# Eight-expert layer of a decoder trunk: gather, scatter and one-hot transposes cut into single steps between blocks of products

## The chip, the cores and the metric

The kernel runs on one core of a Trainium2 chip. The metric is the device time of one execution in microseconds (us); the time before is the median of three executions. Engines are named as the profile names them: PE is TensorE (PEld its weight loads), DVE is VectorE, ACT is ScalarE, POOL is GpSimd, SP is SyncE, which issues the weight loads from memory.

## What is computed

A two-layer decoder trunk on 256 tokens of width 1024. The change lies in the second layer's channel mixer alone, a mixture of eight experts with two experts for each token:

```python
def moe_swiglu(x, w_router, w_gate, w_up, w_down):
    ...
    gates = jnp.sum(jax.nn.one_hot(top_i, N_EXPERTS, dtype=jnp.float32) * top_w[..., None], axis=1)
    y = jnp.zeros((B * S, D), jnp.float32)
    for e in range(N_EXPERTS):
        y = y + gates[:, e:e + 1] * swiglu(xt, w_gate[e], w_up[e], w_down[e]).astype(jnp.float32)
    return y.astype(x.dtype).reshape(B, S, D)
```

`swiglu` is `(silu(x @ w_gate) * (x @ w_up)) @ w_down`, with an inner width of 3584. All numbers are float32.

## The kernel before, in words

**Products.** A float32 weight is split into a rounded part and the rest: ACT writes `whi` (L151), DVE writes `wlo` = weight - `whi` (L152), 128x2048 elements at a time. Three `whi` and three `wlo` buffers exist, so a split waits until PE has used the one three before it. The activations are split in the same way.

**Blocks.** `gate_up(e, m)` takes 512 of an expert's 3584 inner columns: two gate splits, two up splits (g0, g1, u0, u1 below), and after it `down(e, m-1)` takes the two splits d0, d1 of the down matrix of the block before. So a block, written (e, m) with e from 0 to 7 and m from 0 to 6, has six splits on ACT and on DVE and three groups of products on PE; (e, 0) ends with the last `down` of expert e-1. An expert with at most 64 tokens takes the branch `light()` in `either` (16 products for each group, lines L870 and L943 and a `fold` product L836), the others `heavy()` (24 for each group, L161 to L163). With these inputs experts 0, 3, 5 and 6 are heavy and 1, 2, 4 and 7 light, as the lines on PE show; expert 0 has no branch.

**Small work in a block.** ACT: `silu` of the gate bank (L892), the copies `fl` for the fold (L849), half of the transposed inner activations (`wk<-ht`, L915). DVE: `hh` = up times silu (L898) and the other half `wk` (L917). PE: four transposes `ht` (L166). `defer(n, fn)` puts a function on the list `later`; `msplit` takes 2 off n for every 128x2048 split and calls what has reached 0, so such a copy stands behind a later split on its engine's queue.

**Work of an expert or a pair.** `gather(pr)` makes the one-hot masks `pm` of two experts and their inputs `xg` by products with the masks (`gx`, L741): 8 half parts of 4 products, each into one PSUM bank, of which DVE copies the columns of the first expert (L747) and ACT those of the second (L749). It is called whole at the end of block (e, 3) of an odd expert. `gather2` turns the masks round (`gsb`, L790 and L792), copies the gates' column on DVE (`gs`, L793) and the turned masks on ACT (`pTm`, L794). `scaled` and `scatter` multiply the expert's result by its gate (ACT L964, DVE L965, written into `wk`) and add it to the tokens' rows by 8 products (`sc`, L973 and L974) and 4 additions on DVE (`r<-r,sc`, L979); `post` calls it in the middle of block (e+1, 1), before `turn` writes `wk` again.

**PSUM.** The pool `acc` has four banks: two hold an expert's `y` all the time, the other two serve `ht`, `gx`, `gsb` and `sc` in turn. The Tile framework orders each engine's instructions and sets all semaphores; in the built program ACT's copy of a bank waits for DVE's copy of the same bank (`xg` L749 for L747, `pTm` for `gs`).

Of the kernel before, what the change touches and what calls it, by code (L numbers as in the profile page):

```python
# [46 lines left out]
SILU_N, MULT_N, HT_N, FOLD_N = 4, 4, 4, 2  # L47
# [39 lines left out]
def trunk(ctx: ExitStack, tc: tile.TileContext, x, consts, mconsts, vecs, lnrows, w_in, w_uq, w_ukv, w_o,  # L87
# [549 lines left out]
    def moe(pool, raws2, raws3, r, gb, rw):  # L637
# [87 lines left out]
        def gather(pr):  # L725
            pm = pool.tile([P, 2, 256], F32R, tag="pm", name="pm")
            for tt in range(2):
                for j in range(2):
                    ip = nc.vector.tensor_scalar(pm[:, tt, j * P:(j + 1) * P], iota, posm[:, tt, 2 * pr + j:2 * pr + j + 1],
                                            None, ALU.is_equal)  # L730
            if pr == 0:
                hold_splits(((), None, 2), ((pw,), nc.gpsimd, 2), ((i1, pw), nc.gpsimd, 1), ((i1, ip), None, 3))
            xgs = [pool.tile([P, KD, P, 2], F32R, tag="xg", name="xg", bufs=3) for j in range(2)]

            def part(k2):
                for hl, src in enumerate((xth, xtl)):
                    b = bank(acc, "gx")
                    for kk in range(2):
                        k = 2 * k2 + kk
                        for tt in range(2):  # L740
                            nc.tensor.matmul(b[:, kk * 256:(kk + 1) * 256], src[:, tt, k * P:(k + 1) * P], pm[:, tt, :],  # L741
                                             start=(kk == 0 and tt == 0), stop=(kk == 1 and tt == 1))
# [8 lines left out]
            return pm, xgs, part  # L751
# [26 lines left out]
        def gather2(pr, pm, xgs):  # L778
            gs = pool.tile([P, 2], F32, tag="gs", name="gs")
            pT = pool.tile([P, 2, 2, P], F32R, tag="pTm", name="pTm")  # L780

# [5 lines left out]
            for j in range(2):  # L787
# [5 lines left out]
                nc.vector.tensor_copy(gs[:, j:j + 1], b[:, 256 + 2 * pr + j:257 + 2 * pr + j])  # L793
                nc.scalar.copy(pT[:, j, :, :], b[:, 0:256].rearrange("p (a b) -> p a b", b=P))  # L794
            return [(gs[:, j:j + 1], pT[:, j]) for j in range(2)]
# [3 lines left out]
        def defer(n, fn):  # L799
            later.append([n, fn])  # L800
# [37 lines left out]
        def gate_up(e, m, xg, part=None, mid=None):  # L838
# [12 lines left out]
            for g, w in enumerate((e_gate, e_up)):  # L851
# [29 lines left out]
                if dyn:  # L881
                    if g == 0 or (e, m) != LAST:
                        defer(FOLD_N, lambda g=g: copy_for_fold(g))
                    else:
                        copy_for_fold(g)
                if g == 0:
# [7 lines left out]
                    defer(SILU_N + dyn, silu)  # L894
# [64 lines left out]
        def scaled(yb, gs, swap):  # L959
            ys_ = []  # L960
            for n in range(2):
                o = 1024 * (n if swap else 1 - n)
                yh, yl = [wk[:, o + 512 * i:o + 512 + 512 * i] for i in range(2)]
                nc.scalar.activation(yh, yb[n], AF.Copy, scale=gs)  # L964
                nc.vector.scalar_tensor_tensor(yl, yb[n], gs, yh.bitcast(F32), ALU.mult, ALU.subtract)  # L965
                ys_.append((yh, yl))
            return ys_

        def scatter(e, ys_, pT):
            for n in range(2):  # L970
                for tt in range(2):
                    b = bank(acc, "sc")
                    nc.tensor.matmul(b, pT[:, tt, :], ys_[n][0], start=True, stop=False)  # L973
                    nc.tensor.matmul(b, pT[:, tt, :], ys_[n][1], start=False, stop=True)  # L974
                    if e == NE - 1:
                        ln_sum(ya[tt], ya[tt], {n: b}, fsums[tt], 1.0, (n,))
                    else:
                        cs = slice(n * 512, (n + 1) * 512)
                        nc.vector.tensor_tensor(ya[tt][:, cs], ya[tt][:, cs], b, ALU.add)  # L979
# [79 lines left out]
        post = prev = None  # L1059
# [6 lines left out]
        def finish(e, m, ht, fold_up=None, fe=None, hook=None):  # L1066
            nonlocal post
# [3 lines left out]
            if m == FM - 1:  # L1071
                gs, pT = sc[e // 2][e % 2]
                ys_ = scaled(yb[e], gs, e == NE - 1)
                post = lambda: scatter(e, ys_, pT)

        for e in range(NE):
            pr = e // 2
            for m in range(FM):

                def mid():  # L1080
                    nonlocal post
# [14 lines left out]
                if prev is not None:  # L1096
                    h2 = [ht[0]]

# [4 lines left out]
                    finish(*prev[:2], ht[0], fold_up, e, hook if (e, m) == LAST else None)  # L1103
                if m == 3 and e == NE - 1:
# [3 lines left out]
                if m == 3 and e % 2 == 1 and e < NE - 1:  # L1108
                    half[pr + 1] = gather(pr + 1)
                    for k2 in range(4):  # L1110
                        half[pr + 1][2](k2)
                prev = (e, m, hh)
        finish(*prev[:2], h2[1])
        post()
# [248 lines left out]
```

## Time and profile before

| what | us |
|---|---|
| median of three executions | 1484.8 (1484.56 to 1489.42) |
| the profiled execution | 1489.02 |
| its span | 1486.9 |
| PE busy | 1368.8 (92%) |
| DVE busy | 1177.1 (79%) |
| ACT busy | 994.1 (67%) |

The table's last four rows are one execution, taken by the hardware profiler; a share of busy time is an average over stages with different limits. The expert stage lies between about 490 and 1472 us of the span. The rows further down are read block by block: each window begins at one group of PE's products and ends at the same group of the next block.

### The profile page before, as it was taken

What the parts mean: (1) busy time and instruction counts of PE and PEld (TensorE: products, weight loads), DVE (VectorE), ACT (ScalarE), POOL (GpSimd) and SP (SyncE); (2) the same over time, 40 slices, a digit from 0 to 9 for tenths busy, and PEclk for the clock granted to TensorE, in tenths of its full rate; (3) what the DMA queues carried; (4) which work ended last, traced back from release to release, by engine and by line L of the source; (5) the groups of instructions that cost most, each with busy time, mean ns of one, the idle gap of its engine ahead of it and who ended that gap; (6) DMA issues with size and microseconds to landing.
All of it is one profiled execution on the core that took longest, in us unless ns stands there. A gap on an engine that the chain in (4) does not pass through costs nothing. (4 is left out here: it accounts for less than half of the span.)

```text
span 1486.9 us, 18580 instructions
## 1 busy us (share of the span) xinstructions
PE 1368.8 (92%) x6927; PEld 1131.7 (76%) x6927; DVE 1177.1 (79%) x1264; ACT 994.1 (67%) x1065; POOL 79.8 (5%) x113
## 2 busy tenths in 40 slices
PE   7999999999998899988889998998989899999895
PEld 6987999998986788766666777876668787887663
DVE  6577655556667888898999976889987787888996
ACT  3564444445655677777879865778867677778884
POOL 3012000003103000000000000000000000001001
PEclk8999999999999999999999999999999999999997
DMA  6733554544525789998999987989999797999980
GB/s 258 276 132 113 199 197 174 197 144 146 207 86 227 256 327 359 374 380 322 419 372 419 419 321 268 355 331 397 419 368 345 258 367 288 358 367 372 357 351 30
DMA packets 63513, 429.46 MB, mean 289 GB/s; under 512 B 7058, under 2 KB 7570, under 8 KB 15268
## 3 DMA queue, kind: packets, MB, share of 16 engines
q1 hardware_dynamic: 63364, 427.81, 75.1%
q8 instruction: 81, 1.33, 0.4%
q14 instruction: 36, 0.29, 0.1%
q0 software_dynamic: 32, 0.03, 0.0%
HBM read 426.76 MB, written 1.05 MB: 288 GB/s over the span
## 5 line engine op out<-in xcount | busy, mean ns | idle before, releaser
L152 DVE TENSOR_TENSOR wlo<-raw,whi 128x2048 fp32r<-128x2048 f32 (+4 forms) x475 | 910.3, 1937 | 170.5 <-ACT whi L151 164.9
L151 ACT CAST whi<-raw 128x2048 fp32r<-128x2048 f32 (+4 forms) x482 | 772.3, 1619 | 295.3 <-PE eg L163 45.5
L871 PE MATMUL eg<-wlo,xg 128*128 128x512 f32 x448 | 182.5, 407 | 11.6 <-DVE wlo L152 9.5
L162 PE MATMUL eg<-wlo,xg 128*128 128x512 f32 x448 | 179.4, 400 | 7.7 <-DVE wlo L152 7.7
L161 PE MATMUL eg<-whi,xg 128*128 128x512 f32 x448 | 181.0, 404 | 0.0
L870 PE MATMUL eg<-whi,xg 128*128 128x512 f32 x448 | 179.7, 401 | 0.8 <-ACT wk L915 0.8
L163 PE MATMUL eg<-whi,xg 128*128 128x512 f32 x448 | 178.6, 399 | 0.0
L871 PEld LDWEIGHTS eg<-wlo,xg 128*128 128x128 f32 x448 | 85.2, 190 | 45.5 <-DVE wlo L152 29.4
L162 PEld LDWEIGHTS eg<-wlo,xg 128*128 128x128 f32 x448 | 88.3, 197 | 25.3 <-DVE wlo L152 8.6
L943 PE MATMUL y<-wlo,wk 128*128 128x512 f32 x224 | 95.7, 427 | 11.3 <-DVE wlo L152 10.0
L163 PEld LDWEIGHTS eg<-whi,xg 128*128 128x128 f32 x448 | 88.1, 197 | 17.7
L161 PEld LDWEIGHTS eg<-whi,xg 128*128 128x128 f32 x448 | 88.3, 197 | 16.7
L584 PE MATMUL gu<-xhi,whi 128*128 128x256 f32 x352 | 99.8, 283 | 0.1
L585 PE MATMUL gu<-xlo,whi 128*128 128x256 f32 x352 | 99.7, 283 | 0.2 <-DVE xlo L224 0.2
L586 PE MATMUL gu<-xhi,wlo 128*128 128x256 f32 x352 | 99.6, 283 | 0.0
L870 PEld LDWEIGHTS eg<-whi,xg 128*128 128x128 f32 x448 | 85.3, 190 | 17.0 <-ACT wk L915 1.0
L943 PE MATMUL y<-whi,wk 128*128 128x512 f32 x224 | 91.3, 407 | 2.8 <-DVE wk L917 1.5
L162 PE MATMUL y<-wlo,wk 128*128 128x512 f32 x224 | 88.5, 395 | 0.0
L161 PE MATMUL y<-whi,wk 128*128 128x512 f32 x224 | 88.2, 395 | 0.3 <-ACT hh L892 0.3
L163 PE MATMUL y<-whi,wk 128*128 128x512 f32 x224 | 88.2, 394 | 0.0
L943 PEld LDWEIGHTS y<-wlo,wk 128*128 128x128 f32 x224 | 45.0, 201 | 37.4 <-DVE wlo L152 30.1
L584 PEld LDWEIGHTS gu<-xhi,whi 128*128 128x128 f32 x352 | 67.6, 192 | 0.7 <-DVE xlo L224 0.3
(307 smaller groups left out, 2120.6 us busy)
## 6 DMA issues: line engine op xcount, KB each, us to landing
raw<-in_e_gate SPq DMA_DIRECT2D x112, 1024.0 KB, 7.3
raw<-in_e_up SPq DMA_DIRECT2D x110, 1024.0 KB, 7.1
raw<-in_e_down SPq DMA_DIRECT2D x108, 1024.0 KB, 7.4
raw<-in_ffn_gu SPq DMA_DIRECT2D x22, 1024.0 KB, 4.9
raw<-in_ffn_dn SPq DMA_DIRECT2D x11, 1024.0 KB, 4.6
raw<-in_w_in SPq DMA_DIRECT2D x10, 960.0 KB, 4.6
raw<-in_w_o SPq DMA_DIRECT2D x8, 1024.0 KB, 6.8
gb<-in_lnrows SPq DMA_DIRECT2D x8, 512.0 KB, 4.8
```

Of the source, the lines that this page charges most:

```text
L151: last[0] = nc.scalar.copy(hi[:, :n], src)
L152: last[1] = (eng or nc.vector).tensor_tensor(lo[:, :n], src, hi.bitcast(F32)[:, :n], ALU.subtract)
L161: nc.tensor.matmul(o, ahi, bhi, start=start, stop=False)
L162: nc.tensor.matmul(o, ahi, blo, start=False, stop=False)
L163: return nc.tensor.matmul(o, alo, bhi, start=False, stop=stop)
L584: nc.tensor.matmul(o, hi[:, cs], xhi[:, k, :], start=(g == 0 and k == 0), stop=False)
L585: nc.tensor.matmul(o, hi[:, cs], xlo[:, k, :], start=False, stop=False)
L586: nc.tensor.matmul(o, lo[:, cs], xhi[:, k, :], start=False, stop=(g == 1 and k == 7))
L870: nc.tensor.matmul(bs[g], x2, sp[k // 4][0][:, cs], start=(k == 0), stop=False)
L871: nc.tensor.matmul(bs[g], x2, sp[k // 4][1][:, cs], start=False, stop=(k == 7))
L943: nc.tensor.matmul(yb[n], h2, sp[j // 2][i][:, j % 2 * D + n * 512:j % 2 * D + n * 512 + 512], start=(m == 0 and j == 0 and i == 0), stop= ...
```

## The change

The gather, the one-hot transposes and the scatter become single steps on a list `chores`. `point()` is called three times in a block (in `mid` between gate and up, at the end of `gate_up`, after `finish`) and takes at most one step off the list: the 4 products of one half part of a gather, the products of one expert's mask, or the 2 products of one quarter of a scatter. The copies of a step are deferred by `CHORE_N = 2`, that is behind the next split. `scaled` writes into a tile `ys` of its own, in a buffer of the tag `xg`. In blocks with a branch `silu` and `hh` are deferred by 7 units (before 5), and the copies `fl` by 4 (before 2).

```diff
-SILU_N, MULT_N, HT_N, FOLD_N = 4, 4, 4, 2
+HT_N, CHORE_N = 4, 2
...
+            def half_part(k2, hl, n=0):
+                src = (xth, xtl)[hl]
+                b = bank(acc, "gx")
...
+                def copies():
                     bv = b.rearrange("p (a b) -> p a b", b=256)
                     for j in range(2):
                         o = xgs[j][:, 2 * k2:2 * k2 + 2, :, hl]
...
+                defer(n, copies)
...
+            def one(j):
                 b = bank(acc, "gsb")
...
+                def copies():
+                    nc.vector.tensor_copy(gs[:, j:j + 1], b[:, 256 + 2 * pr + j:257 + 2 * pr + j])
+                    nc.scalar.copy(pT[:, j, :, :], b[:, 0:256].rearrange("p (a b) -> p a b", b=P))
+
+                defer(CHORE_N, copies)
...
+        def point():
+            points[0] += 1
+            if chores and chores[0][0] <= points[0]:
+                chores.pop(0)[1]()
...
-                        defer(FOLD_N, lambda g=g: copy_for_fold(g))
+                        defer(4, lambda g=g: copy_for_fold(g))
...
-                    defer(SILU_N + dyn, silu)
+                    defer(7 if dyn else 4, silu)
...
-                defer(MULT_N + dyn, mult)
+                defer(7 if dyn else 4, mult)
...
+                defer(CHORE_N, lambda: nc.vector.tensor_tensor(ya[tt][:, cs], ya[tt][:, cs], b, ALU.add))
...
+                    yt = pool.tile([P, 2, 2, 512], F32R, tag="xg", name="ys", bufs=3)
...
+                    defer(4, both)
+                    for n in range(2):
+                        for tt in range(2):
+                            chores.append((points[0] + 3, lambda n=n, tt=tt: scatter(n, tt, ys[n], pT)))
...
+            chores.extend([(0, first), (0, lambda: one[0](1))])
...
+            chores.append((0, first))
+            chores.extend((0, lambda i=i: half[pr][3](i // 2, i % 2, CHORE_N)) for i in range(1, 8))
...
+                if m == 2 and e % 2 == 0:
+                    prepare_scatter(pr)
+                if m == 2 and e % 2 == 1 and e < NE - 1:
+                    prepare_gather(pr + 1)
...
-                    if post is not None:
-                        post()
-                        post = None
-                    if m == 1 and e % 2 == 0:
-                        sc[pr] = gather2(pr, *half[pr][:2])
+                    point()
```

The lines of the changed kernel: `xg` on DVE L749 and on ACT L751, `hh` L925, `silu` L919, `fl` L876, `wk` L945 and L943, `ys` L988 and L989, the addition L999, the branches L856 and L982.

**ACT, the gather of the second pair, block (3, 3).** Before:

```order
L749 CAST xg<-gx 128x256
L151 CAST whi<-raw 128x2048
L915 CAST wk<-ht 128x4x128
L849 CAST fl<-eg 128x512
L151 CAST whi<-raw 128x2048
L829 UNCONDITIONAL_BRANCH
L749 CAST xg<-gx 128x256 x2
L151 CAST whi<-raw 128x2048
```

The same place after the change, from u1 on; it stands so in (3, 3) and (3, 4), and in (3, 2) with the later pair of copies alone:

```order
L751 CAST xg<-gx 128x256
L151 CAST whi<-raw 128x2048
L943 CAST wk<-ht 128x4x128
L876 CAST fl<-eg 128x512
L151 CAST whi<-raw 128x2048
L856 UNCONDITIONAL_BRANCH
L751 CAST xg<-gx 128x256 x2
L151 CAST whi<-raw 128x2048
```

The three `whi` are u1, d0 and d1. The copies stand at the same two places in the block, now three of them in each of two blocks and two in one, where before all eight stood in (3, 3).

**DVE, the scatter of expert 2 in block (3, 1).** Before:

```order
L898 TENSOR_TENSOR hh<-eg,hh 128x512
L152 TENSOR_TENSOR wlo<-raw,whi 128x2048
L965 SCALAR_TENSOR_TENSOR wk<-y,gs,wk 128x512
L829 UNCONDITIONAL_BRANCH
L965 SCALAR_TENSOR_TENSOR wk<-y,gs,wk 128x512
L979 TENSOR_TENSOR r<-r,sc 128x512 x4
L152 TENSOR_TENSOR wlo<-raw,whi 128x2048 x2
```

After:

```order
L989 SCALAR_TENSOR_TENSOR ys<-y,gs,ys 128x512 x2
L152 TENSOR_TENSOR wlo<-raw,whi 128x2048
L999 TENSOR_TENSOR r<-r,sc 128x512
L152 TENSOR_TENSOR wlo<-raw,whi 128x2048
L945 TENSOR_TENSOR wk<-ht,wk 128x4x128
L856 UNCONDITIONAL_BRANCH
L152 TENSOR_TENSOR wlo<-raw,whi 128x2048 x2
L856 UNCONDITIONAL_BRANCH
L152 TENSOR_TENSOR wlo<-raw,whi 128x2048
L999 TENSOR_TENSOR r<-r,sc 128x512 x2
L152 TENSOR_TENSOR wlo<-raw,whi 128x2048
```

The four additions, one behind the other before, stand behind u0, behind the next block's g0 (two) and, not shown, behind its u0.

**PE, the change of blocks (6, 3) to (6, 4), where nothing is gathered or scattered.** Before (`y` is the end of the light branch of `down`, `eg_10669` the next gate bank):

```order
L943 MATMUL y_10247<-wlo_10614,wk_5038 128x512
L829 UNCONDITIONAL_BRANCH
L166 MATMUL ht_10725<-mc_70,hh_10482 128x128 x4
L829 COMPARE_AND_BRANCH
L161 MATMUL eg_10669<-whi_10675,xg_9319 128x512
```

After, later in the same block (`eg_10673` is the gate bank, `eg_10674` the up bank); `down` is now followed by the gate's branch at once:

```order
L897 MATMUL eg_10673<-whi_10683,xg_9136 128x512
L898 MATMUL eg_10673<-wlo_10684,xg_9136 128x512
L856 UNCONDITIONAL_BRANCH
L166 MATMUL ht_10729<-mc_70,hh_10477 128x128 x4
L856 COMPARE_AND_BRANCH
L161 MATMUL eg_10674<-whi_10738,xg_9136 128x512
```

The transposes move from between `down` and gate to between gate and up; `hh` on DVE moves with them, from behind g0 to behind g1.

## Rows read from the trace of the kernel before

**Rows 1.** Stretches of undisturbed blocks: (0, 5), light (1, 5), heavy (3, 5); columns in the header.
```profile
core 0: us, PE busy (x) PEld busy (x) DVE busy (x) ACT busy (x) POOL busy (x), PEclk, DMA share, GB/s
579.93:597.00 17.07, 17.07 (x77) 14.17 (x76) 14.83 (x9) 12.42 (x8) 0.00 (x0) 1.00 0.95 369
697.65:712.21 14.56, 13.17 (x55) 9.50 (x55) 14.50 (x9) 12.95 (x11) 0.00 (x0) 1.00 1.00 414
938.48:955.79 17.31, 17.29 (x76) 14.08 (x76) 14.67 (x9) 13.28 (x10) 0.00 (x0) 1.00 0.96 362
```
**Rows 2.** Stretches of (4, 0), (3, 0) and (6, 0), up to the first `sc`.
```profile
973.12:989.58 16.46, 14.73 (x62) 10.97 (x62) 15.04 (x9) 13.70 (x12) 0.00 (x0) 1.00 1.00 380
835.19:852.12 16.93, 15.84 (x69) 12.74 (x69) 14.28 (x8) 13.14 (x12) 0.00 (x0) 1.00 1.01 419
1222.96:1241.39 18.43, 17.58 (x77) 14.15 (x77) 15.22 (x9) 13.91 (x12) 0.00 (x0) 1.00 0.96 357
```
**Rows 3.** Stretches of (e, 1), from the first `sc` on, e from 1 to 7.
```profile
624.95:643.61 18.66, 15.50 (x63) 10.96 (x63) 18.66 (x16) 14.33 (x12) 0.00 (x0) 1.00 0.85 314
741.63:762.44 20.81, 16.98 (x79) 12.91 (x79) 18.91 (x21) 14.99 (x14) 0.00 (x0) 1.00 0.90 355
852.12:876.01 23.89, 20.93 (x85) 16.74 (x85) 18.79 (x16) 13.79 (x11) 0.00 (x0) 0.93 0.80 308
989.58:1010.59 21.01, 17.99 (x78) 14.18 (x78) 18.87 (x21) 15.17 (x14) 0.00 (x0) 0.92 0.76 293
1100.33:1124.31 23.98, 21.01 (x84) 16.72 (x84) 18.82 (x16) 13.79 (x11) 0.00 (x0) 0.93 0.82 311
1241.39:1264.46 23.07, 21.28 (x100) 17.55 (x100) 18.17 (x17) 14.44 (x13) 0.00 (x0) 1.00 0.68 251
1368.00:1388.39 20.39, 15.91 (x62) 12.42 (x63) 17.84 (x15) 14.97 (x12) 0.00 (x0) 0.92 0.80 304
```
**Rows 4.** Stretches of the gather's blocks (1, 3), (3, 3), (5, 3), and of (5, 4).
```profile
658.16:683.09 24.93, 18.58 (x87) 14.83 (x87) 18.46 (x21) 15.70 (x19) 0.00 (x0) 0.93 0.89 348
893.33:921.18 27.85, 23.22 (x108) 19.39 (x109) 18.47 (x21) 16.55 (x19) 0.00 (x0) 0.94 0.74 276
1141.64:1169.48 27.84, 23.21 (x108) 19.29 (x109) 18.45 (x21) 16.50 (x19) 0.00 (x0) 0.94 0.74 274
1169.48:1188.31 18.83, 18.80 (x77) 15.20 (x77) 14.59 (x9) 12.19 (x10) 0.00 (x0) 0.91 0.72 265
```
**Rows 5.** Timeline of DVE in (1, 3): start, us, engine line operation, count, idle time before and releaser.
```profile
662.42 0.42 DVE L747 CAST xg<-gx 128x256 fp32r<-128x256 f32 x1
...
665.08 2.29 DVE L152 TENSOR_TENSOR wlo<-raw,whi 128x2048 fp32r<-128x2048 f32 x1 [0.57 <-ACT whi L151]
```
**Rows 6.** Timeline of ACT at the same place.
```profile
662.87 0.38 ACT L749 CAST xg<-gx 128x256 fp32r<-128x256 f32 x1 [3.60 <-DVE xg L747]
663.14 1.90 ACT L151 CAST whi<-raw 128x2048 fp32r<-128x2048 f32 x1
```
**Rows 7.** Timeline of PE in the gather of (3, 3).
```profile
905.96 0.63 PE L741 MATMUL gx<-pm,xth 128*128 128x256 f32 x4
906.42 0.64 PE L741 MATMUL gx<-pm,xtl 128*128 128x256 f32 x4
...
910.58 0.91 PE L741 MATMUL gx<-pm,xtl 128*128 128x256 f32 x4 [2.32 <-ACT xg L749]
```
**Rows 8.** Timeline of PE in (3, 1), behind the scatter.
```profile
863.51 0.80 PE L162 MATMUL eg<-wlo,xg 128*128 128x512 f32 x1 [2.94 <-DVE wlo L152]
864.11 0.63 PE L163 MATMUL eg<-whi,xg 128*128 128x512 f32 x1
864.53 0.63 PE L161 MATMUL eg<-whi,xg 128*128 128x512 f32 x1
```
**Rows 9.** Timeline of DVE in (3, 1): the additions of the scatter.
```profile
858.78 2.48 DVE L979 TENSOR_TENSOR r<-r,sc 128x512 f32<-128x512 f32 x4 [2.79 <-PE sc L974]
```

More of the change, by code (lines that the diff above doesn't have):

```diff
@@ L733, in gather @@
             xgs = [pool.tile([P, KD, P, 2], F32R, tag="xg", name="xg", bufs=3) for j in range(2)]
[L735 to L742, printed above, removed]
+            def half_part(k2, hl, n=0):
+                src = (xth, xtl)[hl]
+                b = bank(acc, "gx")
+                for kk in range(2):
+                    k = 2 * k2 + kk
+                    for tt in range(2):
+                        nc.tensor.matmul(b[:, kk * 256:(kk + 1) * 256], src[:, tt, k * P:(k + 1) * P], pm[:, tt, :],
+                                         start=(kk == 0 and tt == 0), stop=(kk == 1 and tt == 1))
+                def copies():
                     bv = b.rearrange("p (a b) -> p a b", b=256)
@@ L749, in part @@
                             nc.scalar.copy(o, bv[:, :, P:256])
-            return pm, xgs, part
+                defer(n, copies)
+            def part(k2):
+                for hl in range(2):
+                    half_part(k2, hl)
+            return pm, xgs, part, half_part
         def counts():
@@ L776, in weights, with gather2 @@
             posds.append(posd)
[L778 removed]
+        def gather2(pr, pm):
             gs = pool.tile([P, 2], F32, tag="gs", name="gs")
             pT = pool.tile([P, 2, 2, P], F32R, tag="pTm", name="pTm")
+            sc[pr] = [(gs[:, j:j + 1], pT[:, j]) for j in range(2)]
             for j in range(2):
@@ L957, in down, with scaled, scatter @@
                 hook()
[L959 to L979, printed above, removed]
+        def scaled(n, yb, gs, y):
+            nc.scalar.activation(y[0], yb[n], AF.Copy, scale=gs)
+            nc.vector.scalar_tensor_tensor(y[1], yb[n], gs, y[0].bitcast(F32), ALU.mult, ALU.subtract)
+        def scatter(n, tt, y, pT, last=False):
+            b = bank(acc, "sc")
+            nc.tensor.matmul(b, pT[:, tt, :], y[0], start=True, stop=False)
+            nc.tensor.matmul(b, pT[:, tt, :], y[1], start=False, stop=True)
+            if last:
+                ln_sum(ya[tt], ya[tt], {n: b}, fsums[tt], 1.0, (n,))
+            else:
+                cs = slice(n * 512, (n + 1) * 512)
+                defer(CHORE_N, lambda: nc.vector.tensor_tensor(ya[tt][:, cs], ya[tt][:, cs], b, ALU.add))
         def ln_rows_bc2():
@@ L1072, in finish, with both, prepare_scatter, first @@
                 gs, pT = sc[e // 2][e % 2]
-                ys_ = scaled(yb[e], gs, e == NE - 1)
-                post = lambda: scatter(e, ys_, pT)
+                if e == NE - 1:
+                    ys = [[wk[:, 1024 * n + 512 * i:1024 * n + 512 * i + 512] for i in range(2)] for n in range(2)]
+                    for n in range(2):
+                        scaled(n, yb[e], gs, ys[n])
+                    for n in range(2):
+                        for tt in range(2):
+                            scatter(n, tt, ys[n], pT, True)
+                else:
+                    yt = pool.tile([P, 2, 2, 512], F32R, tag="xg", name="ys", bufs=3)
+                    ys = [[yt[:, n, i] for i in range(2)] for n in range(2)]
+                    def both():
+                        for n in range(2):
+                            scaled(n, yb[e], gs, ys[n])
+                    defer(4, both)
+                    for n in range(2):
+                        for tt in range(2):
+                            chores.append((points[0] + 3, lambda n=n, tt=tt: scatter(n, tt, ys[n], pT)))
+        def prepare_scatter(pr):
+            one = []
+            def first():
+                one.append(gather2(pr, half[pr][0]))
+                one[0](0)
+            chores.extend([(0, first), (0, lambda: one[0](1))])
+        def prepare_gather(pr):
+            def first():
+                half[pr] = gather(pr)
+                half[pr][3](0, 0, CHORE_N)
+            chores.append((0, first))
+            chores.extend((0, lambda i=i: half[pr][3](i // 2, i % 2, CHORE_N)) for i in range(1, 8))
         for e in range(NE):
```

23 lines of the change are left out of this document (10 added, 13 removed).

## Prediction

> **What bounds the kernel now.** I read the share of busy time first (PE 92%, DVE 79%), and then did not use it, because the expert stage has two kinds of blocks with different limits. The sums over stretches show this. In a heavy block PE is busy for 17.29 of 17.31 us, DVE for 14.67: PE is the bound, and DVE has 2.6 us to spare. In a light block DVE is busy for 14.50 of 14.56 us, PE for 13.17: DVE is the bound, and every microsecond in which it waits is lost [rows 1]. A block of expert 0, which has no branch and whose transposes stand between gate and up, takes 17.07 us, 0.24 less than a heavy block of the others [rows 1].
>
> Next I looked for the blocks that are longer than these. They are (e, 1), with the scatter and every second time the turned masks [rows 3], and the three blocks with a gather [rows 4]. Over the undisturbed length of their kind these lose 4.1, 6.3, 6.6, 6.5, 6.7, 5.8 and 5.8 us in rows 3, and 10.4, 10.5 and 10.5 in rows 4, with another 1.5 in (5, 4): some 75 us in all. That is what the change can win, less what the moved work must still cost.
>
> Last come the timelines, for the price of one wait. DVE's copy of a gather bank ends at 662.84. ACT's copy of the same bank starts at 662.87, the `whi` queued behind it at 663.14, and DVE can begin `wlo` at 665.08 [rows 5, 6]. So wherever an ACT copy stands ahead of a split, the next `wlo` starts 2.24 us after the end of DVE's copy, and ends 2.29 later. In the scatter the four additions take 2.48 us, after 2.79 of waiting for the products [rows 9], and PE then waits 2.94 for DVE [rows 8].
>
> **The order after the change.** The list of instructions shows that the steps really are where the diff says. But it also shows ACT's copies ahead of u1 in two blocks and ahead of d1 in three for each gather, each waiting for a DVE copy that stands behind the `wlo` of the split before. ACT may therefore not run ahead of DVE at five places, where it needs to.
>
> **Term 1, ordinary heavy blocks.** The transposes no longer follow `down`, where they waited for `hh`; a heavy block becomes as short as one of expert 0. Experts 3, 5 and 6 have six such blocks each, m from 1 to 6: 18 x 0.24 = 4.3 us less. Bounds: 0, if the branches cost the 0.24, and 4.3. I take 4.3, as both kinds have the same products. In light blocks DVE does the same work in another order, so nothing changes.
>
> **Term 2, entry blocks (e, 0)** [rows 2]. They end in a wait of PE for the scaled result. (3, 0) and (5, 0) have 64 products instead of 72; at the pace of expert 0 that is 17.07 x 64/72 = 15.2, with the fold 15.4 instead of 16.93, so 1.5 less each. (6, 0) comes to 17.4 instead of 18.43, 1.0 less. (1, 0), (4, 0) and (7, 0) lie between DVE's 14.56 and today's 16.46; I take the middle, 15.6, 0.9 less each. Sum: 3.0 + 1.0 + 2.7 = 6.7 less; bounds 2 and 9.
>
> **Term 3, scatter and turned masks.** In a light expert DVE must still do four additions and two scalings, 6 x 0.62 = 3.7 [rows 9], and waits about 0.4 where two additions follow four `sc` products: 4.1. In a heavy one PE must do 8 products of 17.07/72 = 0.24 us, 1.9, and DVE comes late by an estimated 0.9 for the next split: 2.8. The masks have a step of the same kind as the gather: a copy of ACT ahead of d1, 2.24 us of DVE's time, with the wait of the first mask products for a bank (1.0) and the two copies 3.5 in a light block; in a heavy one 4.4, as PE must also do the 16 small products (about 1.8). So: (1, 1) from 4.1 to 4.1; (7, 1) from 5.8 to 4.1; (3, 1) and (5, 1) from 6.6 and 6.7 to 2.8; (2, 1) and (4, 1) from 6.3 and 6.5 to 7.6; (6, 1) from 5.8 to 7.2, the new cost spread over two blocks. Sum: 0 - 1.7 - 7.7 + 2.4 + 1.4 = 5.6 less. Bounds: 0 for a full wait at each addition, 12 with no wait for masks.
>
> **Term 4, gather.** *Light, in (1, 2) to (1, 4).* DVE makes eight copies of 0.42 [rows 5], 3.4 us, and now waits at five places: three times 2.24 ahead of d1; twice 2.24 - 0.42 = 1.8 ahead of u1, where it has a second copy to make; and once about 0.7, because the first products need the bank of an addition. Together 3.4 + 6.7 + 3.6 + 0.7 = 14.4 instead of 10.4 us: 4.0 more. *Heavy, in (e, 2) to (e, 4).* Four products take 0.46 [rows 7]. Ahead of d1 the chain is: four products behind up, DVE's copy 0.42, then 2.24, then 2.29 until `wlo` is there, 4.95 us; PE meanwhile has 12 products of d0, 2.7, so it waits 2.2. Ahead of u1 the second four products wait for both copies of the first (0.42 + 0.38 [rows 5, 6] and a little, 0.9), and u1 itself comes 0.75 late. So (e, 2) gets 2 x 0.46 + 0.65 for the bank + 2.2 = 3.8 and the two others 3 x 0.46 + 0.9 + 0.75 + 2.2 = 5.2 each, 14.2 instead of 10.5 (3.7 more), and with (5, 4) 12.0 (2.2 more). Sum: 9.9 more. Bounds: if none of the five waits were left, a gather would cost 3.4 on DVE or 3.8 + 0.65 on PE, in all some 19 less; the other bound is 16 more, with each wait half as long again.
>
> Here a rule of the notes can be set beside the rows. The row shows ACT's copy starting 0.03 us after the end of DVE's, never beside it [rows 5, 6]. The Trainium skill, "PSUM — Partial Sum Buffer", section "Specifications (TRN2)", says that ScalarE and VectorE can read PSUM in parallel at full bandwidth as long as there is no bank collision; its section "PSUM bank collisions raise a hardware error" counts two readers of one bank as such a collision. By the first sentence alone the copies would not wait and the total would fall by some 30 us; by the second, with which the row agrees, they must stand one behind the other, as in my sum.
>
> **Term 5, the first pair's masks** move from (0, 1) into (0, 2) and (0, 3) with the same 16 products and two copies. No row prices that; between 1 less and 4 more (two waits of 2.2 ahead of `whi`), I take 1 more, as expert 0 has the spare time of a heavy block on DVE.
>
> **Term 6, the clock of PE.** After the wait of 2.94 us products start 0.43 apart [rows 8] instead of 0.24, which is the level of 1.2 GHz. The granted clock of that stretch is 0.93 [rows 3], so about 14% of its 23.9 us ran at half speed and cost 1.7 us. A wait of 2.32 also led to slow products (0.91 instead of 0.64 for four [rows 7]), yet (2, 1) and (6, 1) kept a clock of 1.00 [rows 3]. The change leaves two such places fewer in scatters, counted in term 3, and makes seven waits of about 2.2 in heavy blocks. I count between two and three of them at 1.7, 4 us more; bounds 0 and 12.
>
> **Sum.** -4.3 - 6.7 - 5.6 + 9.9 + 1 + 4 = -1.7 us. The profiled execution took 1489.0 us, 4.2 more than the median of the three runs; set against the median of 1484.8, the sum gives **1483.1 us**. A measurement of this kernel can tell about 0.5%, 7.4 us, from no change, so I forecast no change.
>
> **Rivals.** *Faster: the waits lie in spare time.* DVE has 2.6 us to spare in a heavy block [rows 1]. If the splits there run one further ahead than my chain has it, the wait ahead of d1 is covered, PE pays for its products alone, and each heavy gather costs 4.5 instead of 14.2, the masks of expert 6 lose 2.2, and the slow clock of term 6 goes: 19.4 + 2.2 + 4 = 26 less, 1457; with half of it covered 1470. For it: the kernel loses 75 us in work that now stands between blocks. Against it: three buffers bind a split to the product three splits before, and at five places ACT stands behind DVE. The Trainium skill, "Perfetto Trace Analysis", section "Optimization Strategy", says that interleaving regimes with different contended engines may improve performance; by that rule this rival is the outcome. I give 0.32.
>
> *Slower: the clock falls after every wait.* If a wait of 2.2 us in a heavy block is enough each time, seven waits cost 12 instead of 4, and in the light blocks, where PE stands still for some 3 us ahead of d1, the late products free their buffers late, about 0.6 at each of seven places, 4 more: 1483.1 + 8 + 4 = 1495. It decides from about five falls in seven. For it: the slow products after 2.32 us [rows 7] and the clock of 0.91 in (5, 4) [rows 4]. Against it: the stretches at 1.00. I give 0.20.
>
> **Numbers.** No change has 0.48 (its own range is 1477 to 1492), faster 0.32, slower 0.20. The range reaches into both rivals, to the half-covered waits with a part of term 2's bound, and just past the slower case: 1463 to 1497.
>
> **What would show it.** Right: ACT's `xg` waits for DVE's `xg` in sum at least as long as before; DVE waits for `whi` some 2.2 us ahead of d1 in (1, 2) to (1, 4), each of which lasts 18 to 20 us; blocks (3, 3) and (3, 4) last about 22 us; ordinary heavy blocks last 17.07, and the idle time of PE before `ht` is gone; (3, 1) lasts about 20 with a clock of 1.00. Wrong: heavy gather blocks below 19 us (then faster), a clock under 0.95 over each of them (then slower), or an ordinary light block that is not 14.56.

## The result and the profile after

The changed kernel takes 1505.35 us (median of 4 runs, 1503.68 to 1506.69); the kernel before, run beside it, 1484.68 (4 runs, 1482.30 to 1489.42). The ratio is **1.0135, 95% interval 1.0107 to 1.0162**: slower, where no change was forecast, and above the range. The profiled execution took 1503.68 us, with a span of 1501.7 against 1486.9, so 14.8 us of the difference can be followed in the two traces. DVE and ACT did almost the same work (busy 1180.8 and 995.9 us, against 1177.1 and 994.1).

The stretches below answer to [rows 1] and [rows 4]: the undisturbed light block (2, 5) and heavy block (3, 5), then the blocks that now share the gather, (1, 3) and (3, 2) to (3, 4). Each goes from the first product of gate to the next block's; the columns are those of [rows 1].

```profile
817.57:831.97 14.40, 13.49 (x56) 9.49 (x54) 14.40 (x9) 12.96 (x10) 0.00 (x0) 1.00 1.01 420
...
952.57:969.65 17.08, 17.08 (x77) 14.10 (x76) 14.98 (x10) 13.38 (x10) 0.00 (x0) 1.00 0.97 356
...
663.87:685.37 21.50, 16.78 (x67) 12.50 (x66) 16.32 (x13) 13.89 (x13) 0.00 (x0) 0.90 0.79 304
...
881.74:905.60 23.86, 21.16 (x88) 16.36 (x86) 18.66 (x14) 13.12 (x12) 0.00 (x0) 0.93 0.80 289
905.60:929.86 24.26, 21.16 (x89) 16.66 (x88) 15.93 (x12) 13.99 (x13) 0.00 (x0) 0.93 0.71 261
929.86:952.57 22.71, 19.60 (x90) 15.50 (x88) 15.32 (x15) 14.01 (x13) 0.00 (x0) 1.00 0.69 249
```

Undisturbed blocks are shorter, as forecast for heavy ones. But three blocks of 22.7 to 24.3 us, 70.8 together, stand where before three of 62.5 together stood. In them neither PE nor DVE is busy all the time, so they wait for one another. The next fences follow one gather step in (3, 3). DVE, with the idle time ahead of an instruction and its releaser in brackets:

```profile
920.65 0.43 DVE L749 CAST xg<-gx 128x256 fp32r<-128x256 f32 x1 [0.60 <-PE gx L741]
923.32 2.29 DVE L152 TENSOR_TENSOR wlo<-raw,whi 128x2048 fp32r<-128x2048 f32 x1 [2.25 <-ACT whi L151]
```

ACT at the same place:

```profile
921.11 0.39 ACT L751 CAST xg<-gx 128x256 fp32r<-128x256 f32 x1 [3.12 <-DVE xg L749]
921.39 1.90 ACT L151 CAST whi<-raw 128x2048 fp32r<-128x2048 f32 x1
```

And PE:

```profile
923.34 0.50 PE L161 MATMUL y<-whi,wk 128*128 128x512 f32 x1
925.67 0.79 PE L162 MATMUL y<-wlo,wk 128*128 128x512 f32 x1 [1.83 <-DVE wlo L152]
926.26 0.63 PE L163 MATMUL y<-whi,wk 128*128 128x512 f32 x1
926.69 0.63 PE L161 MATMUL y<-whi,wk 128*128 128x512 f32 x1
```

This is the chain of [rows 5, 6], now in the middle of `down`: DVE's copy ends at 921.08, ACT's starts at 921.11, `whi` of d1 at 921.39, `wlo` at 923.32, and PE, which has gone through d0, starts the next product 2.33 us after the last instead of 0.23. Behind it products start 0.43 apart instead of 0.23, the level of 1.2 GHz. The waits of ACT, summed over the span (columns: us in total, times, longest), show that this happens at more places and lasts longer (idle time of ACT alone is not yet lost time; the blocks above show what is lost). Before:

```profile
ACT xg L749 <- DVE xg L747: 27.3, 13, 3.8
```

After:

```profile
ACT xg L751 <- DVE xg L749: 64.8, 19, 5.3
```

**Where the time went.** The starts of gate's first products, read from the two traces, give the length of each stretch; the table shows the difference to before in us, beside the prediction's terms 1 to 5 for the stretch (0.24 of term 1 to each heavy block from m = 1 on). The other columns belong to experiments below: the gather in one piece, the transposes alone, and the last version.

| blocks | predicted | changed | gather whole | transposes alone | all tied, DVE |
|---|---|---|---|---|---|
| (0, 2) to (0, 5), first masks | +1.0 | +1.9 | +1.9 | 0.0 | +1.9 |
| (0, 6) to (1, 1), scatter | -0.9 | -2.1 | -2.1 | -0.4 | -2.1 |
| (1, 2) to (1, 5), gather | +4.0 | **+8.7** | +1.1 | +0.5 | -2.7 |
| (1, 6) | 0.0 | 0.0 | -0.1 | -0.2 | -0.1 |
| (2, m), scatter, masks | +1.3 | +2.6 | +2.6 | -0.8 | +0.1 |
| (3, 0), (3, 1), scatter | -5.5 | -5.4 | -5.4 | 0.0 | -5.7 |
| (3, 2) to (3, 4), gather | +3.0 | **+8.4** | +0.9 | -0.3 | -6.5 |
| (3, 5), (3, 6) | -0.5 | -0.5 | -0.5 | -0.5 | -0.5 |
| (4, m), scatter, masks | +0.2 | +2.1 | +2.2 | -1.1 | -0.4 |
| (5, 0), (5, 1), scatter | -5.6 | -5.6 | -5.6 | -0.2 | -5.8 |
| (5, 2) to (5, 4), gather | +1.5 | **+6.9** | -0.5 | -0.4 | -8.0 |
| (5, 5), (5, 6) | -0.5 | -0.5 | -0.5 | -0.5 | -0.5 |
| (6, m), scatter, masks | -1.0 | -0.9 | -0.9 | -1.7 | -4.5 |
| (7, 0) to (7, 5), scatter | -2.6 | -1.6 | -1.6 | -1.3 | -1.9 |
| sum | -5.6 | +13.9 | -8.6 | -6.8 | -36.8 |

Term 6, the clock, was counted separately with 4 more. The three gathers alone cost 24.0 us more than before, the other stretches 10.1 less.

### The profile page after: what moved, and what is told of

Same layout as the page of the kernel before. It is cut to its first block, busy times and chain, and to the rows that moved or that the text cites. A ratio compares the mean times of both kernels' runs of the same rounds, so it can differ in the third digit from the quotient of the medians.

```text
span 1501.7 us, 18572 instructions
## 1 busy us (share of the span) xinstructions
PE 1378.6 (92%) x6927; PEld 1129.2 (75%) x6927; DVE 1180.8 (79%) x1264; ACT 995.9 (66%) x1065; POOL 79.6 (5%) x113
## 5 line engine op out<-in xcount | busy, mean ns | idle before, releaser
L898 PEld LDWEIGHTS eg<-wlo,xg 128*128 128x128 f32 x448 | 84.8, 189 | 72.7 <-DVE wlo L152 57.2
L971 PE MATMUL y<-wlo,wk 128*128 128x512 f32 x224 | 98.3, 439 | 19.3 <-DVE wlo L152 18.1
L162 PE MATMUL y<-wlo,wk 128*128 128x512 f32 x224 | 90.8, 405 | 13.0 <-DVE wlo L152 13.0
L971 PE MATMUL y<-whi,wk 128*128 128x512 f32 x224 | 94.0, 420 | 5.8 <-ACT whi L151 3.1
L161 PE MATMUL y<-whi,wk 128*128 128x512 f32 x224 | 90.5, 405 | 0.3 <-ACT hh L919 0.3
L163 PE MATMUL y<-whi,wk 128*128 128x512 f32 x224 | 89.9, 401 | 0.0
```

The lines of the kernel that those rows point to most:

```text
L161: nc.tensor.matmul(o, ahi, bhi, start=start, stop=False)
L162: nc.tensor.matmul(o, ahi, blo, start=False, stop=False)
L163: return nc.tensor.matmul(o, alo, bhi, start=False, stop=stop)
L898: nc.tensor.matmul(bs[g], x2, sp[k // 4][1][:, cs], start=False, stop=(k == 7))
L971: nc.tensor.matmul(yb[n], h2, sp[j // 2][i][:, j % 2 * D + n * 512:j % 2 * D + n * 512 + 512], start=(m == 0 and j == 0 and i == 0), stop= ...
```

## Experiments

The theory at the start: the loss is the gather's steps, where ACT stands behind DVE ahead of a split. Rivals: the scatter and masks, now spread over two blocks (B); copies that come too soon behind their products, whichever engine makes them (C); for the masks alone, that they cost only their products and copies, and no wait (D); later, that what helps is a tie to a split and not the engine (E). The expectations call the theory A. Times are medians; the kernel before took 1487.65, 1486.61 and 1487.40 beside the three groups of four runs, so ratios are what to compare.

**1. The gather in one piece again.**

```diff
-                if m == 2 and e % 2 == 1 and e < NE - 1:
-                    prepare_gather(pr + 1)
+                if m == 3 and e % 2 == 1 and e < NE - 1:
+                    half[pr + 1] = gather(pr + 1)
+                    for k2 in range(4):
+                        half[pr + 1][2](k2)
```

Expected: 

> The changed kernel with the gather whole again, in one piece behind down of (1, 3), (3, 3), (5, 3); masks, scatter and transposes stay in steps. Theory A (the loss lies in the steps of the gather, where ACT's copy of a bank stands ahead of a split and waits for DVE's copy): the gather's blocks lose 18 to 19 us per expert in steps against 10.4 to 12 in one piece, so 7 to 8 us less at each of three places, about 23 less than the changed kernel: 1482. Rival B (the loss lies in the scatter and the masks, now spread over two blocks): the gather's steps are worth nothing either way, 1500 to 1505.

Measured: 1480.87, ratio 0.9944 (0.9919 to 0.9969). The stretch (3, 2) to (3, 4):

```profile
874.13:892.27 18.14, 18.05 (x79) 14.33 (x78) 16.35 (x12) 12.66 (x10) 0.00 (x0) 1.00 0.88 331
892.27:919.85 27.58, 23.53 (x110) 19.35 (x109) 17.47 (x15) 15.22 (x17) 0.00 (x0) 0.94 0.78 291
919.85:937.52 17.67, 17.36 (x79) 14.14 (x77) 15.97 (x14) 13.66 (x11) 0.00 (x0) 1.00 0.73 272
```

These are 63.4 us where the steps need 70.8. Over the three gathers the table gives 22.5 us; all else stays as in the changed kernel. The loss is the gather's steps, and rival B falls.

**2. The masks in one piece as well.**

```diff
-            chores.extend([(0, first), (0, lambda: one[0](1))])
+            chores.append((0, first))
...
-                defer(CHORE_N, copies)
+                copies()
```

(`first` then calls both masks.) Expected: 

> As the first, and the turned masks in one piece too (both banks at one point, copied at once): what is left of the change is the scatter in steps and the transposes between gate and up. Theory A: one more pair of ACT-behind-DVE waits is gone in experts 0, 2, 4 and 6, about 1 us each: 1478, with (1, 1) and (7, 1) unchanged. Rival B: if the scatter itself is the loss, still above 1495.

Measured: 1480.82, ratio 0.9949 (0.9932 to 0.9967), as the first. It decides nothing: the list of instructions shows the masks moved in (0, 2) and (0, 3) alone; for the later pairs they were placed where they had been.

**3. Both gather copies on DVE.**

```diff
-                        if j == 0:
-                            nc.vector.tensor_copy(o, bv[:, :, 0:P])
+                        if j == 0 or n:
+                            nc.vector.tensor_copy(o, bv[:, :, j * P:(j + 1) * P])
```

Expected: 

> The changed kernel with both copies of a gather bank on DVE, none on ACT. Theory A: ACT no longer waits for DVE ahead of u1 and d1. In a heavy block the chain from the gather products to the wlo of d1 is 0.42 + 0.42 + 2.29 = 3.1 instead of 4.95 us against 2.7 us of products of d0, so PE's wait falls from 2.33 to about 0.5, the slow clock behind it goes and blocks (3, 3), (3, 4) fall from 24.3 to about 20; in light blocks DVE pays 0.42 in place of 2.24, 21.0 becomes about 18. In all 25 less: 1480. Rival C (what counts is that the copies come one split behind their products, whichever engine makes them): DVE still stands behind the products, PE's wait of 2.33 stays above 1.5 and the time is 1498 or more.

Measured: 1482.24, ratio 0.9964 (0.9947 to 0.9981). The wait ahead of d1 is gone and the time is as the theory gives it; the blocks are not quite, (3, 3) and (3, 4) taking 22.40 and 20.85, the first at a granted clock of 0.92. PE's rows ahead of up in (3, 3) show why:

```profile
903.71 0.71 PE L741 MATMUL gx<-pm,xth 128*128 128x256 f32 x4
905.36 0.71 PE L741 MATMUL gx<-pm,xtl 128*128 128x256 f32 x4 [0.94 <-DVE xg L749]
907.02 0.71 PE L741 MATMUL gx<-pm,xth 128*128 128x256 f32 x4 [0.94 <-DVE xg L749]
```

The order had changed too: all three steps of a block now stand ahead of up, and the second and third wait for the copies of the one before. So this run alone doesn't separate the engine from the place.

**4. Everything put off by two splits.**

```diff
-HT_N, CHORE_N = 4, 2
+HT_N, CHORE_N = 4, 4
```

Expected: 

> The changed kernel with all copies and additions put off by two splits instead of one. Theory A: ACT's copy still stands ahead of a split and waits for DVE's, so DVE's wait of 2.24 stays at as many places: light gather blocks stay at 21 us; in heavy ones the wait moves to a split that PE needs later, so 24.3 falls to about 21 as DVE's own 14.7 + 1.3 + two waits of about 2.2. In all some 12 less: 1493. Rival C: with two splits between products and copies nobody waits: light gather blocks about 16.5, heavy ones about 18.5, 1478.

Measured: 1502.41, ratio 1.0088 (1.0062 to 1.0114). The edit did nothing: the order of instructions on PE, DVE and ACT is the changed kernel's, row for row. A copy without a tie of its own is not placed by the splits that the program counts. So the run tests neither theory; it is a repeat of the changed kernel, useful for the clock and for the noise: the same order of instructions gave 1.0135 the first time and 1.0088 here, so between runs of different groups a difference of this size shows nothing by itself. Its blocks (3, 3) and (3, 4):

```profile
905.07:927.75 22.68, 19.58 (x89) 15.49 (x88) 14.53 (x11) 13.99 (x13) 0.00 (x0) 1.00 0.69 251
927.75:951.94 24.19, 21.09 (x89) 16.42 (x88) 18.08 (x17) 13.99 (x13) 0.00 (x0) 0.93 0.80 287
```

In the changed kernel's execution it was the first of the two that ran at 0.93. The same wait of PE (1.83 and 1.82 us in the two (3, 3)) brought the clock down in one and not in the other.

**5. Both gather copies on ACT.** The theory has two readings: ACT's wait for DVE's copy of the same bank, or ACT standing ahead of a split and waiting for anything late.

```diff
-                        if j == 0:
+                        if j == 0 and not n:
                             nc.vector.tensor_copy(o, bv[:, :, 0:P])
                         else:
-                            nc.scalar.copy(o, bv[:, :, P:256])
+                            nc.scalar.copy(o, bv[:, :, j * P:(j + 1) * P])
```

Expected: 

> The changed kernel with both copies of a gather bank on ACT, none on DVE; PE's order and the places of ACT's copies stay as in the changed kernel. Theory A in its narrow form (the loss is ACT's wait for DVE's copy of the same bank): that wait is gone, as in the run with both copies on DVE, 1482. Theory A in its wide form (the loss is that ACT stands ahead of a split, waiting for anything late, since whi and wlo follow one behind the other): ACT now waits for the products of PE; from them to the wlo of d1 are 0.4 + 0.4 + 1.9 + 2.29 = 5.0 us against 2.7 of d0, so PE's wait ahead of d1 stays at about 2.3, blocks (3, 3) and (3, 4) at 24 and light ones at 20 to 21: 1500.

Measured: 1503.49, ratio 1.0115 (1.0086 to 1.0144), no better than the changed kernel. ACT, then DVE, then PE ahead of d1 in (3, 3):

```profile
920.22 0.66 ACT L751 CAST xg<-gx 128x256 fp32r<-128x256 f32 x2 [2.38 <-PE gx L741]
920.76 1.91 ACT L151 CAST whi<-raw 128x2048 fp32r<-128x2048 f32 x1
```

```profile
922.71 2.29 DVE L152 TENSOR_TENSOR wlo<-raw,whi 128x2048 fp32r<-128x2048 f32 x1 [3.08 <-ACT whi L151]
```

```profile
925.05 0.50 PE L162 MATMUL y<-wlo,wk 128*128 128x512 f32 x1 [1.83 <-DVE wlo L152]
```

No copy of DVE is left, and PE waits 1.83 us as before. The wide reading holds: wherever ACT must wait ahead of a split, `whi` and `wlo` follow it in series.

**6. Masks on DVE too.**

```diff
-                    nc.scalar.copy(pT[:, j, :, :], b[:, 0:256].rearrange("p (a b) -> p a b", b=P))
+                    nc.vector.tensor_copy(pT[:, j, :, :], b[:, 0:256].rearrange("p (a b) -> p a b", b=P))
```

Expected: 

> Gather copies and the copy of the turned masks all on DVE. Theory A: besides the gather, the masks' pair of waits in (0, 2), (0, 3), (2, 2), (4, 2), (6, 2) and the blocks behind them goes, 1.5 to 2 us at each step of eight: some 10 less than with the gather copies alone, 1472. Rival D (the masks cost their 16 products and DVE's copies, no wait): 1481 to 1484.

Measured: 1474.28, ratio 0.9931 (0.9905 to 0.9956), 8 less than run 3, in the medians and in the two traces. But only 4.9 of the 8 lie in experts 2, 4 and 6, where the masks are: DVE's wait ahead of d1 in (2, 2) falls from 1.46 us in the changed kernel to 0.29, and that block from 21.78 to 19.33. The other 3.1 lie in the two heavy gathers, where the granted clock fell in one block each in run 3 (0.92 in (3, 3) and (5, 2)) and in none in run 6. In (0, 2) to (0, 5) nothing is saved. So the masks of the later pairs paid a price of the gather's kind, about half of what was expected; rival D, no wait at all, falls.

**7. Copies on DVE and tied behind a `wlo`.** Run 6 with the gather's copies tied; the tie is the one that `hh` has:

```diff
-                            nc.vector.tensor_copy(o, bv[:, :, j * P:(j + 1) * P])
+                            with after(*([dve[0]] if n else [])):
+                                nc.vector.tensor_copy(o, bv[:, :, j * P:(j + 1) * P])
```

Expected: 

> As the run before (all copies on DVE), and each gather copy tied behind the wlo issued last before it; the list of instructions then has one gather step between gate and up and two between up and down, where three stood between gate and up. If the loss that is left is PE's wait of 1.22 us between two gather steps at one place, it falls to one such wait per block: 4 to 6 less than the run before. If that wait only moves to the place between up and down, the same time as the run before within 3 us.

Measured: 1459.68, ratio 0.9839 (0.9803 to 0.9875): 15 less than run 6, more than expected. (3, 2) to (3, 4):

```profile
866.70:886.61 19.91, 19.04 (x87) 15.34 (x86) 17.11 (x14) 12.67 (x10) 0.00 (x0) 1.00 0.91 334
886.61:905.13 18.52, 18.52 (x89) 15.59 (x88) 16.76 (x15) 13.39 (x10) 0.00 (x0) 1.00 0.97 349
905.13:923.93 18.80, 18.80 (x90) 15.51 (x88) 17.16 (x18) 13.38 (x10) 0.00 (x0) 1.00 0.87 304
```

PE is busy for all of (3, 3) and (3, 4). The first takes 17.07 and 1.45 for the products of three steps, so the gather is hidden but for its products. The expectation had left one of PE's waits between steps in each block; in these two blocks none is left. From run 6 to run 7 the two heavy gathers get 11.1 us shorter by the traces, the light one 3.4.

**8. The transposes alone**, in the kernel before:

```diff
-SILU_N, MULT_N, HT_N, FOLD_N = 4, 4, 4, 2
+SILU_N, MULT_N, HT_N, FOLD_N = 4, 4, 4, 4
...
-                    defer(SILU_N + dyn, silu)
+                    defer(7 if dyn else 4, silu)
...
-                defer(MULT_N + dyn, mult)
+                defer(7 if dyn else 4, mult)
```

Expected: 

> The kernel before with nothing but the three delays of silu, product and fold copy of the changed one (7, 7 and 4 splits): the transposes go between gate and up, gather, masks and scatter stay in one piece. Term 1 of the prediction: heavy blocks 17.07 instead of 17.32, light ones unchanged; 20 heavy blocks, some 5 us less than before. Rival: the scatter, which now stands in two pieces around gate, gives it back, no change.

Measured: 1482.44, ratio 0.9974 (0.9958 to 0.9991), 4.2 less. The light block (2, 5) and the heavy (3, 5):

```profile
803.72:818.14 14.42, 13.53 (x56) 9.50 (x54) 14.42 (x9) 12.96 (x10) 0.00 (x0) 1.00 1.01 419
935.56:952.63 17.07, 17.07 (x77) 14.18 (x76) 14.86 (x9) 13.38 (x10) 0.00 (x0) 1.00 0.96 369
```

17.07 is what term 1 said. Light blocks get 0.14 shorter too, which it had excluded.

**9. Tied, but divided between DVE and ACT as in the changed kernel** (DVE's copy tied behind `wlo` as in run 7, ACT's behind `whi`; the masks' copies on ACT):

```diff
+                            with after(*([last[0]] if n else [])):
+                                nc.scalar.copy(o, bv[:, :, P:256])
```

Expected: 

> The changed kernel with DVE's gather copies tied behind the wlo and ACT's behind the whi issued last before them; the copies stay divided between DVE and ACT, masks as in the changed kernel. Theory A in its wide form: between each pair of splits with a copy ACT waits for DVE's copy, and the next wlo starts 2.24 us behind it; with three copies to a block DVE needs 14.5 + 3 x 2.66 = 22.5 us, so gather blocks last 22 to 24, light or heavy: 1500 to 1510. Rival E (what helped in the last run but one was the tie behind the split, not the engine): heavy gather blocks 18.5, light ones 16 to 17: 1465.

Measured: 1501.34, ratio 1.0092 (1.0069 to 1.0115). DVE from (3, 2) into (3, 3), rows with copies and what follows them:

```profile
902.05 0.42 DVE L750 CAST xg<-gx 128x256 fp32r<-128x256 f32 x1
904.72 2.29 DVE L152 TENSOR_TENSOR wlo<-raw,whi 128x2048 fp32r<-128x2048 f32 x1 [2.24 <-ACT whi L151]
...
909.72 0.42 DVE L750 CAST xg<-gx 128x256 fp32r<-128x256 f32 x1
912.38 2.29 DVE L152 TENSOR_TENSOR wlo<-raw,whi 128x2048 fp32r<-128x2048 f32 x1 [2.24 <-ACT whi L151]
```

The copies' products are long done (DVE starts each copy without a wait), and still every copy costs 2.24 us. So rival C's distance from the products is not what matters here, and rival E, the tie alone, falls: with the tie, the engine decides. In this variant the narrow reading is the one that bites, ACT waiting for DVE's copy.

**10 to 12. Towards the shortest version.** Run 10 ties the masks' copies in the same way, run 11 the scatter's additions, run 12 also puts the first half of the scaled result on DVE (not for the last expert); shown are the additions and the scaling:

```diff
+                def add():
+                    with after(dve[0]):
+                        nc.vector.tensor_tensor(ya[tt][:, cs], ya[tt][:, cs], b, ALU.add)
+
-                defer(CHORE_N, lambda: nc.vector.tensor_tensor(ya[tt][:, cs], ya[tt][:, cs], b, ALU.add))
+                defer(CHORE_N, add)
...
-        def scaled(n, yb, gs, y):
-            nc.scalar.activation(y[0], yb[n], AF.Copy, scale=gs)
+        def scaled(n, yb, gs, y, e):
+            (nc.vector.tensor_scalar(y[0], yb[n], gs, None, ALU.mult) if e < NE - 1 else nc.scalar.activation(y[0], yb[n], AF.Copy, scale=gs))
...
```

Expected of run 10: 

> The run with all copies on DVE and the gather's copies tied, and the masks' two copies tied behind a split too; the masks' products then stand as one step between gate and up and one between up and down. Theory: PE's wait between the two mask steps (about 1.2 us) goes in (2, 1) and later even experts: 2 to 4 less, 1456 to 1458. If nothing waits there, the same.

Expected of run 11: 

> As the run before, and the scatter's additions tied behind a split as well. Heavy experts 3 and 5: DVE's waits for the scatter's products ahead of an addition (1.17 and 1.03 us) and PE's 1.17 behind them go, about 1 to 2 each; light experts the same: in all 4 to 8 less, 1450. If the scatter's cost is DVE's own work, the same within 3 us.

Expected of run 12: 

> As the run before, and both halves of the scaled result on DVE, none on ACT. Theory A in its wide form also holds for ACT's two scalings, which stand ahead of a split and wait for the last products of down: DVE's wait of 2.39 us in (e, 1) of light experts goes, and DVE pays two operations of about 0.65: 1 us less for each of 4 light experts, 4 less. Rival: DVE's added work costs what the wait did, no difference within 3 us.

Measured: 1456.38 (ratio 0.9796, 0.9773 to 0.9818), **1451.39 (0.9755, 0.9729 to 0.9781)** and 1459.02 (0.9806, 0.9780 to 0.9832). The first two came as expected; their intervals overlap, but by the traces the stretches of the table are 5.1 shorter in run 11 than in run 10. Run 11 is 2.45% shorter than the kernel before; its (1, 3) and (3, 3):

```profile
659.41:675.86 16.45, 14.08 (x67) 11.31 (x66) 16.45 (x15) 13.23 (x10) 0.00 (x0) 1.00 1.00 385
...
885.86:904.38 18.52, 18.52 (x90) 15.59 (x89) 16.76 (x15) 13.38 (x10) 0.00 (x0) 1.00 0.93 339
```

DVE is busy for all of the light one, PE for all of the heavy one. Run 12 is a miss: 7.6 us slower than run 11. DVE's wait behind the entry to expert 1, which I had put down to ACT's scalings, is still there (2.41 in run 12), and DVE pays 1.40 more:

```profile
624.89 4.50 DVE L152 TENSOR_TENSOR wlo<-raw,whi 128x2048 fp32r<-128x2048 f32 x2 [2.41 <-ACT whi L151]
...
629.91 1.40 DVE L991 TENSOR_SCALAR ys<-y,gs 128x512 fp32r<-128x512 f32 x2
```

The changed kernel's ACT shows what that wait is: `whi` waits for products of `down` there, and the scalings come behind it.

```profile
622.13 3.71 ACT L151 CAST whi<-raw 128x2048 fp32r<-128x2048 f32 x2 [2.42 <-PE y L163]
625.75 1.25 ACT L988 ACTIVATE ys<-y,gs 128x512 fp32r<-128x512 f32 x2
```

## Why the prediction was wrong

**Term 1, ordinary heavy blocks: right.** 17.07, or 0.25 less, in each undisturbed one. That light blocks gain nothing was wrong by 0.14 each; run 8 shows that this comes with the transposes, and why was not tried. Term 5, the first pair's masks, had 1 more; 1.9 were measured.

**Terms 2 and 3, entry and scatter: near in the blocks that they name.** In experts 3 and 5 -5.4 and -5.6, forecast -5.5 and -5.6; in experts 1 and 7 -2.1 and -1.6, forecast -0.9 and -2.6. But the end of the scatter now runs on into (e, 2), where it is counted below (1.1 us in experts 3 and 5, 1.6 in expert 1). The masks of light experts were priced too low: experts 2 and 4 together +4.7, forecast +1.5. With their copies on DVE too, in run 6, it is +1.1.

**Term 4, gather: right mechanism, too small; with term 6 the step that failed.** In the table the gathers come out at +24.0, where the prediction had 8.5 for them and 4 for the clock. The whole table differs from its predicted column by 19.5 us: 8.0 are the clock in the heavy gathers, 3.6 waits of DVE in the light one, 3.2 the masks of experts 2 and 4, and the other 4.7 are spread, the scatter's end among them. Heavy: (3, 2) to (3, 4) last 70.8, 19.6 over three blocks of 17.07, of which 1.1 is the scatter's end ((3, 2) of run 1 lasts 18.1). Of the other 18.5 the clock is 4.0 (the three `down` take 9.44, 9.41 and 7.85 us against 5.45 for an undisturbed one, 2.10 of each being the wait). What is left, 14.5, is what term 4 said, 14.2. Light: (1, 2) to (1, 5) last 77.3, 19.7 over four blocks of 14.41, 1.6 of it the scatter's end; 18.0 where term 4 had 14.4. DVE in (1, 3), up to the first splits of (1, 4), shows two waits that I had not counted:

```profile
669.77 0.43 DVE L749 CAST xg<-gx 128x256 fp32r<-128x256 f32 x1 [0.64 <-PE gx L741]
671.45 0.43 DVE L749 CAST xg<-gx 128x256 fp32r<-128x256 f32 x1 [1.26 <-PE gx L741]
672.44 2.29 DVE L152 TENSOR_TENSOR wlo<-raw,whi 128x2048 fp32r<-128x2048 f32 x1 [0.57 <-ACT whi L151]
...
680.12 2.29 DVE L152 TENSOR_TENSOR wlo<-raw,whi 128x2048 fp32r<-128x2048 f32 x1 [2.25 <-ACT whi L151]
682.89 2.29 DVE L152 TENSOR_TENSOR wlo<-raw,whi 128x2048 fp32r<-128x2048 f32 x1 [0.48 <-ACT whi L151]
```

The 0.64 (DVE reaches the first gather bank before PE has filled it) and the 0.48 behind the long wait are new; the 1.26 and 0.57 together are the 1.8 that term 4 had. The first comes twice and the second three times in the gather, 2.7 of the 3.6 us. What stands ahead of the 0.48 is ACT's own row of work behind its wait, without a gap:

```profile
678.18 1.90 ACT L151 CAST whi<-raw 128x2048 fp32r<-128x2048 f32 x1
679.98 0.60 ACT L919 ACTIVATE hh<-eg 128x512 f32<-128x512 f32 x1
680.47 0.59 ACT L876 CAST fl<-eg 128x512 fp32r<-128x512 f32 x1
680.93 3.73 ACT L151 CAST whi<-raw 128x2048 fp32r<-128x2048 f32 x2
```

**Term 6, the clock: mis-sized.** "Between two and three of seven at 1.7" should have been four of seven at 1.9, for 7 to 8 us: behind four of the six waits in the heavy gathers the clock fell, and (6, 2) with the masks, the seventh, kept 1.00. Two of three fell in each heavy gather, in both executions of this order, but not the same two. The term also left out the light blocks: (1, 3) and (1, 4) ran at a granted clock of 0.90, (2, 2) and (4, 2) at 0.92. A light block's length goes by DVE and its waits, so what the clock costs there can't be read off, and whether it adds to the 0.64 was not tried.

**The rivals.** The slower one came nearest. It had the clock at more waits than the sum, but was to decide only from about five falls in seven, and there were four; it also had some 4 us in light blocks, but from buffers that PE frees late, while the 0.48 has ACT's own work ahead of it. It stopped at 1495, since it left the rest of the sum as it was. The faster one ("the waits lie in spare time") was wrong for this change and right for the one it could have been: with the copies tied, on DVE, (3, 2) to (3, 4) cost 5.0 over blocks of 17.07 and the scatter's end (57.2 - 51.2 - 1.1), and it had said 4.5. That its time, 1457, is near that run's 1459.68 is partly luck: run 7 also has the masks on DVE and a light gather 2.4 us shorter than before, and the rival had left the light gather at 4.0 more. What spoke against it in the prediction, ACT behind DVE at five places, decided.

**Bank collisions and interleaving.** The prediction weighed the Trainium skill, "PSUM — Partial Sum Buffer", section "PSUM bank collisions raise a hardware error": two readers of a bank collide, so copies stand one behind the other. ACT's copy again starts 0.03 us after DVE's ends, but run 5, where one engine reads each bank and nothing is saved, shows that this order was not the whole price. The Trainium skill, "Perfetto Trace Analysis", section "Optimization Strategy", says that interleaving regimes in which different engines are the most contended may help. By itself it did not: 1.0135. It did once the interleaved copies no longer stood in ACT's way: 0.9755 in run 11.

**The signs.** Of those the prediction named as right, ACT's wait for DVE's `xg` (27.3 to 64.8 us), DVE's 2.2 ahead of d1, the 17.07 of heavy blocks and a (3, 1) near 20 with full clock (19.04) are there; the light gather blocks, forecast at 18 to 20, last 20.4 to 21.5, and (3, 3) and (3, 4), forecast at about 22, last 24.3 and 22.7. Of its signs of being wrong, one is there in full, the ordinary light block that is not 14.56 (14.40), and the clock under 0.95 in two of the three heavy gather blocks (0.93, 0.93, 1.00).

**The base.** The sum was set against a median of 1484.8, while its rows came from an execution of 1489.0. Terms 1 to 6 said -1.7; the traces say +14.8, the medians +20.7. So about 6 of the 22 us between forecast and medians are not the terms': the profiled execution of the kernel before lies 4.3 above its median, that of the changed kernel 1.7 below. Two slips in the prediction's working change little: the middle of 14.56 and 16.46 is 15.5, not 15.6, and term 4 without its waits comes to 20 to 21 us less, not 19.

## What to carry to other kernels

Before putting work into the gaps of a pipeline, ask on which engine's queue it will wait and what stands behind it there: 0.4 us of copy at the head of a chain of two engines (1.9 and 2.29 us) held up the chain's second half by 2.2 us each time, while the same copy on the chain's last engine, tied behind a split, left little more than the work itself (17.07 + 1.45 us in a heavy block). Look at the order that is really issued: for these copies a delay counted in splits moved nothing, while a tie to an instruction did, and tying without changing the engine helped just as little. When a change is a bundle, price its parts apart: here the gather's steps lost 24 us, and all the other parts together gained 10.

## What the runs showed of the hardware that was not expected

The clock of PE does not follow from the program's order alone: the same instructions with the same wait (1.83 and 1.82 us) left (3, 3) at a granted clock of 0.93 in one execution and 1.00 in the other, and (3, 4) the other way round, 1.5 us each. So the clock's cost in one block of one trace is not that block's; over a gather it was the same both times, two of three. The spread of one kernel's times goes with it: of the 37 executions of the kernel before that were timed beside the experiments (1482.78 to 1492.46 us), the seven shortest have a mean granted clock of 0.979 to 0.982, the eight longest one of 0.973 to 0.977. What tips a single wait stays open.
